# The last five MLP tiles and the entry of an S5 state space: an order written by hand, a separate residual buffer, a small position table, and a second period's positions issued ahead

## The chip, the cores and the metric

The kernel runs on one core of a Trainium2 chip. The metric is the device time of one execution in microseconds, median over runs. A core has a matrix engine (TensorE, PE in the profile), a vector engine (DVE), a scalar engine with function tables (ACT), GpSimd (POOL) and SyncE (SP), which in this kernel issues the transfers (DMA). Each engine runs its own instructions in the order in which the program lists them, and stands where one of them waits for another engine or a transfer. SBUF is the on-chip memory that the large buffers U, FD, H and W are cut from; PS is the matrix engine's accumulator memory, in banks of 512 fp32 columns.

## The reference

Two layers over 1024 latent tokens and 256 context tokens of width 1024, all in fp32. Layer 0 is a differential attention with a squared-ReLU MLP, layer 1 a bidirectional S5 state space with the same kind of MLP. The change lies at the border between them: the end of layer 0's MLP and the start of layer 1's mixer.

```
# end of layer 0                                   # start of layer 1
x = x + g2 * rmsnorm(mlp(h), norm_g[0, 3])         h_lat = rmsnorm(x, norm_g[1, 0]) * (1 + s1) + sh1
                                                   y = s5_mixer(h_lat, h_ctx, ...)
# s5: per group of 16 channels, a diagonal complex recurrence over time, forward and backward
lam_bar = exp(lam * dt);   h[t] = lam_bar * h[t-1] + b_bar @ u[t];   y[t] = real(c @ h[t])
```

## The kernel before

The 1280 tokens (8 latent tiles of 128, 0 to 7, and 2 context tiles, 8 and 9) go through MLP0's second product in `mlp0_down`: 53 blocks over 112 slices of the inner width, each product as three matrix instructions of 512 columns (`mm3`, L132 to L134). Partial sums are collected in FD (`yacc`, one 4 KB piece per tile), and half of the tiles is finished from the accumulators. Block 52 holds the last eight slices (q from 104 to 111) for five pairs of tiles, in which the tiles 9, 4, 5, 6, 7 come to their end.

A tile's end is the list of steps that `m0_tile` returns. `first` squares the half in the accumulator on ACT (L1712) and multiplies it by the gate row G on DVE (L1713). `root1` takes the reciprocal root on POOL. `residual` (L1726) adds the old residual x, loaded from xa, and stores the new one to xb in four transfers; it is written over the tile's sum y in FD. `second` squares that on ACT (L1731) and multiplies it by row A, on DVE or, for tiles 9 and 5, on POOL (L1732). `root` takes the second root. `modulate` (L1735) writes the result for layer 1 back into y. Then `transposed` (L1694, four quarters for a pair of tiles) turns it into U, from which the S5 reads.

In block 52 these steps are put in by `stages` and `advance`, which issue them in rounds, and the program's scheduler (`schedule_with_timeline_sim`) then reorders each engine's list by its own estimate of times.

The S5 (`s5`) runs 16 periods of 4 pairs of channel groups, for both directions d. A period n makes `phase(n, d)` (a sum of two integer tables, POOL, L1793), `trig(n, d)` (four steps on ACT, L1797 to L1800: the sine and cosine of the position), `inputs` (PE, L1813), `rotate` (two products on DVE, L1822, from the accumulators with the cosine and sine), a sum of both on POOL (L1903 forward, L1912 backward), `scan` (DVE, L1831), `back` (the rotation back, DVE or POOL, L1839) and `outputs` (PE). The scheduler is off here (`self.manual()`) for PE, ACT, DVE and POOL: they run in the written order. The positions of period 0 come from two small tables A0 and B0 (40 KB in all), those of later periods from a large one, ptd of 1664 KB, at FD 42.5. The `stages` calls of the tiles and the S5's opening are separate pieces of code, but run into one another on every engine. An offset such as FD 12 counts KB per partition.

Of the kernel before, what the change touches and what calls it, by code (L numbers as in the profile page):

```python
# [70 lines left out]
class Prog:  # L71
# [1525 lines left out]
    def mlp0_down(self):  # L1597
# [6 lines left out]
        self.bg = [self.s5_phases(40), self.s5_tables(0, self.bank(3), self.bank(2))]  # L1604

# [16 lines left out]
        for blk in range(53):  # L1622
            for q in range(112):
                d = q // 2 - blk
                if q > 3 and (d == 3 or blk == 0 and d < 3):
                    self.mlp0_load(q)
            for q in range(4 if blk == 0 else 2 * blk + 4, min(2 * blk + 6, 112) if blk < 52 else 112):
                self.mlp0_prep(q)
            steps = range(2 * blk, 2 * blk + 2) if blk < 52 else range(104, 112)
            n = steps[0] // 16  # L1630
            if blk == 40:
                self.drain()
                self.mlp0_rows(0)
                for i in range(4):
                    self.stages(self.m0_tile(i), 2)
                for pr in (0, 1):
                    self.stages([lambda pr=pr, c=c: self.transposed(pr, c) for c in range(3)])
            if blk == 48:
                self.advance()
                self.mlp0_rows(1)  # L1640
                self.stages(self.m0_tile(8), 2)
            if blk == 52:
                self.advance()
                for pr in (0, 1):
                    self.transposed(pr, 3)
                for t in range(5):
                    self.m0_early(T[t][1])
            for t in range(5):
                for q in steps:
                    products(q, t)  # L1650
                if steps[-1] % 16 == 15:
                    evac(n, t)
                if blk == 52:
                    i, b = T[t][1:]
                    fns = self.m0_tile(i, self.bank(b))
                    if i in (9, 5, 7):
                        pr = i // 2
                        fns += [lambda pr=pr, c=c: self.transposed(pr, c) for c in range(4)]
# [13 lines left out]
    def m0_buffers(self, i):  # L1672

        f, w = lambda x: self.fv(x, 1024), lambda: self.wv(12, 1024)
        h = lambda: self.hv(52, 1024).bitcast(F32)
# [20 lines left out]
    def m0_tile(self, i, b=None):  # L1696
# [9 lines left out]
        def first():  # L1706
            self.tile_dma(self.xa, i, x)
            if b is None:
                act.activation(junk, y, AF.Square, scale=1.0 / 32, accum_out=ms)
                pool.tensor_tensor(w, y, G, ALU.mult)  # L1710
                return
# [13 lines left out]
        def residual():  # L1725
            v.scalar_tensor_tensor(y, w, r, x, ALU.mult, ALU.add)  # L1726
            if i < 8:
                self.tile_dma(self.xb, i, y, store=True)

        def second():  # L1730
            act.activation(junk, y, AF.Square, scale=1.0 / 32, accum_out=ms)  # L1731
            (pool if i in (9, 5) else v).tensor_tensor(w, y, A, ALU.mult)  # L1732

        def modulate():
            v.scalar_tensor_tensor(y, w, r, B, ALU.mult, ALU.add)  # L1735

        return [first, root1, residual, second, root, modulate]
# [13 lines left out]
    def s5(self):  # L1751
# [14 lines left out]
        cs = [[(self.fv(x, 4, 128), self.fv(y, 4, 128)) for x, y in (((5, 32), (29.5, 34)), ((15, 22.5), (17.5, 22.5)))[d]]  # L1766
# [91 lines left out]

        for t, c0, w in ((A0, 0, 10), (B0, 5 * KB, 16)):
            self.dma(t, self.ptd[:, c0 : c0 + 128 * w].rearrange("p (d x w) -> p d x w", d=2, w=w)[:, :, 0:4])  # L1860

        load_x(0)
        self.dma(self.fv(42.5, 13 * KB).bitcast(I32), self.ptd)
        load_w(0)
        self.act_set("silu_and_others")
        with self.manual():
            act.activation(U[:, :, 160:192], U[:, :, 0:32], AF.Copy)
# [3 lines left out]
            phase(0, 0)  # L1871
            phase(0, 1)
            trig(0, 0)
            decay(0, 0)
            load_x(1)
            load_w(1)
            for n in range(19):
# [9 lines left out]
                if run:  # L1887
                    trig(n, 1)
                    decay(n, 1)
# [19 lines left out]
                if run:  # L1909
# [299 lines left out]
    def run(self):  # L2209
        tc = self.tc  # L2210
        pool = lambda name, **kw: tc.tile_pool(name=name, bufs=1, **kw)
        with pool("cst") as self.cst, pool("psp", space=bass.MemoryType.PSUM) as psp, \
# [53 lines left out]
            with pool("u") as up, pool("fd") as fp:  # L2266
                self.U, self.F = up.tile([128, 62 * KB], F32, name="U"), fp.tile([128, 56 * KB], F32, name="FD")
                self.mlp0_down()
                self.s5()
# [52 lines left out]
```

## Time and profile before

| what | number |
|---|---|
| time, median of 3 runs | 2897.81 us (2890.6 to 2905.84) |
| profiled execution, its own time | 2912.55 us |
| its span | 2910.8 us |
| granted TensorE clock, mean | 0.979 |
| busy: PE, DVE, ACT, POOL | 2747.0, 2024.0, 1366.7, 1070.7 us |
| last product of MLP0 starts | 1844.43 us |
| first product of the S5 starts | 1865.91 us |

The profile is of one execution. A timeline row gives the start, the duration, the engine, the line, the operation and its operands (out<-in), the count, and in brackets how long the engine stood idle before it and what ended that. The chain of waits follows back from the last instruction what each step waited for; its rows are start, length and the engine or transfer. A window's row gives the busy time of each engine in a stretch, the clock granted to TensorE, the share in which the DMA engines were busy, and GB/s.

### The profile page before, as it was taken

The numbers are of one execution on the slowest core, as the hardware profiler recorded it, in microseconds if no ns is written. First come the engines' busy times: TensorE is split into PE (matmuls) and PEld (weight loads), VectorE is DVE, ScalarE is ACT, GpSimd is POOL, SyncE is SP. The second block draws the span as 40 slices with busy tenths as digits, with TensorE's granted clock in tenths as the row PEclk, the third lists the DMA queues.
The fourth block names the chain that finished last, engine by engine and source line by source line (L and its number), as shares of the span: only waits on it lengthen the run. The fifth ranks groups of instructions, "written<-read, shape, count | busy, mean of one in ns | idle before, by whom it ended". The sixth has DMA issues, their size and how long they took to land.

```text
span 2910.8 us, 43626 instructions
## 1 busy us (share of the span) xinstructions
PE 2747.0 (94%) x15201; PEld 2296.5 (79%) x15201; DVE 2024.0 (70%) x2957; ACT 1366.7 (47%) x2556; POOL 1070.7 (37%) x923
## 2 busy tenths in 40 slices
PE   7999999999899999999999899689899899999999
PEld 4687888888777887878777788588788688888887
DVE  5456788777863667766787767699633687758566
ACT  3425555565554743333443435477443543345443
POOL 2314666666663600000100013699220543326324
PEclk9999999999999999999999999899999999999999
DMA  9855555555826468875899877578743254467544
GB/s 299 299 172 168 151 176 172 169 167 164 253 86 192 120 213 310 309 281 187 283 293 275 261 236 224 160 223 282 255 136 107 67 184 157 149 214 254 163 135 142
DMA packets 452010, 588.43 MB, mean 202 GB/s; under 512 B 60622, under 2 KB 297420, under 8 KB 448588
## 3 DMA queue, kind: packets, MB, share of 16 engines
q1 hardware_dynamic: 451788, 585.63, 63.4%
q8 instruction: 120, 1.97, 0.3%
q14 instruction: 102, 0.84, 0.1%
HBM read 398.47 MB, written 182.82 MB: 200 GB/s over the span
## 4 chain that ended last, share of the span: by engine, by line
PE 67%; DMA 12%; DVE 9%; issue 5%; POOL 3%; ACT 3%; SPq 2%; DVEq 0%; ACTq 0%; POOLq 0%
PE PS L132 19%; PE PS L134 19%; PE PS L133 18%; PE PS L523 3%; PE PS L569 2%; SPq L80 2%; PE PS L1813 2%; DMA FU<-in_mlp_w 2%; DMA Ta<-FU 1%; PE PS L1848 1%; DMA U<-Aa 1%; DVE H L138 1%; ACT F L546 1%; PE PS L202 1%; DVE F L557 1%
## 5 line engine op out<-in xcount | busy, mean ns | idle before, releaser
L132 PE MATMUL PS<-H 128*128 128x512 f32 x1048 | 413.8, 396 | 5.8 <-DVE FD L1620 4.0
L134 PE MATMUL PS<-H 128*128 128x512 f32 x1048 | 411.2, 393 | 1.3 <-DVE H L138 1.3
L133 PE MATMUL PS<-H 128*128 128x512 f32 x1048 | 412.0, 393 | 0.0
L132 PE MATMUL PS<-H,R 128*128 128x512 f32 (+1 forms) x836 | 309.6, 376 | 0.7 <-ACT H L137 0.7
L133 PE MATMUL PS<-H,R 128*128 128x512 f32 (+1 forms) x836 | 305.1, 365 | 4.2 <-POOL H L138 4.1
L134 PE MATMUL PS<-H,R 128*128 128x512 f32 (+1 forms) x836 | 303.8, 364 | 0.0
L132 PEld LDWEIGHTS PS<-H 128*128 128x128 f32 x1048 | 198.8, 190 | 51.1 <-DVE FD L1620 4.2
L134 PEld LDWEIGHTS PS<-H 128*128 128x128 f32 x1048 | 198.6, 190 | 44.4 <-DVE H L138 1.7
L133 PEld LDWEIGHTS PS<-H 128*128 128x128 f32 x1048 | 198.8, 190 | 41.5 <-issue 1.2
L137 ACT ACTIVATE R<-W 128x512 fp32r<-128x512 f32 (+1 forms) x199 | 139.0, 705 | 183.3 <-PE PS L133 119.1
L546 ACT ACTIVATE F<-F,stat 128x1280 f32<-128x1280 f32 x128 | 174.3, 1362 | 99.5 <-DVE F L536 99.3
L132 PE MATMUL PS<-R,H 128*128 128x512 f32 x532 | 213.0, 402 | 1.6 <-ACT R L137 1.6
L133 PE MATMUL PS<-R,H 128*128 128x512 f32 x532 | 210.5, 396 | 0.0
L134 PE MATMUL PS<-R,H 128*128 128x512 f32 x532 | 208.8, 396 | 0.0
L137 ACT ACTIVATE H<-U 128x640 fp32r<-128x640 f32 x216 | 133.0, 677 | 156.6 <-PE PS L133 123.6
L138 DVE TENSOR_TENSOR H<-W,H 128x512 fp32r<-128x512 f32 (+1 forms) x137 | 130.1, 960 | 90.6 <-ACT H L137 90.6
L138 DVE TENSOR_TENSOR H<-U,H 128x640 fp32r<-128x640 f32 x216 | 161.3, 783 | 43.1 <-ACT H L137 42.8
L536 DVE TENSOR_SCALAR_CACHE_REDUCE F<-PS 128x1280 f32<-128x1280 f32 x128 | 185.2, 1483 | 8.2 <-PE PS L523 7.9
L138 DVE TENSOR_TENSOR R<-W,R 128x512 fp32r<-128x512 f32 (+1 forms) x164 | 146.2, 899 | 62.9 <-ACT R L137 55.3
L583 POOL TENSOR_SCALAR R<-F 128x256 fp32r<-128x256 f32 (+1 forms) x128 | 128.0, 1000 | 148.7 <-ACT F L582 130.8
L133 PEld LDWEIGHTS PS<-H,R 128*128 128x128 f32 x836 | 161.3, 193 | 26.9 <-POOL H L138 5.9
L132 PEld LDWEIGHTS PS<-H,R 128*128 128x128 f32 x836 | 160.4, 192 | 26.5 <-issue 4.1
(491 smaller groups left out, 6850.5 us busy)
## 6 DMA issues: line engine op xcount, KB each, us to landing
W<-in_mlp_w SPq DMA_DIRECT2D x184, 256.0 KB, 3.0
U<-Aa SPq DMA_DIRECT2D x108, 320.0 KB, 4.5
Aa<-FU SPq DMA_DIRECT2D x91, 320.0 KB, 4.8
Ad<-F SPq DMA_DIRECT2D x112, 256.0 KB, 2.0
W<-Ad SPq DMA_DIRECT2D x112, 256.0 KB, 2.8
FU<-in_mlp_w SPq DMA_DIRECT2D x32, 512.0 KB, 5.5
Ta<-FU SPq DMA_DIRECT2D x16, 1024.0 KB, 4.4
recd<-U SPq DMA_DIRECT2D x64, 256.0 KB, 4.3
```

The costliest lines, as they stand in the source:

```text
L80: return self.nc.sync.dma_start(out=out, in_=in_)
L132: mm(out, ah, bh, start=first, stop=False, **kw)
L133: mm(out, ah, bl, start=False, stop=False, **kw)
L134: mm(out, al, bh, start=False, stop=last, **kw)
L137: self.nc.scalar.activation(hi, src, AF.Copy)
L138: (lo_eng or self.nc.vector).tensor_tensor(lo, src, hi.bitcast(F32), ALU.subtract)
L523: mm(self.PS[:, 1280 * c + k0 : 1280 * c + k1], Q[:, c, r, qs], K[c][:, k0:k1], start=r == 0, stop=r == 1)
L536: ts(p[c], self.PS[:, 1280 * c : 1280 * c + 1280], 1.0, None, ALU.mult, ALU.min, accum_out=sm[:, c : c + 1])
L546: nc.scalar.activation(p[c], p[c], AF.Exp, bias=sm[:, c : c + 1], scale=-1.0, accum_out=sn[:, 0:1] if c else s0[:, u + 1 : u + 2])
L569: self.nc.tensor.transpose(tb[:, 128 * (kt - k0) : 128 * (kt - k0) + 128], w[:, 128 * kt : 128 * kt + 128], self.ident)
L583: nc.gpsimd.tensor_scalar(hi, t, 1.0, 0.0, ALU.mult, ALU.add)
L1813: mm(b[:, o : o + 160], X[:, d, i, 64 * j : 64 * j + 128], U[:, 4 * n + i, cols], start=True, stop=True)
```

## The change

Block 52 no longer goes through `stages` and `advance`. `mlp0_end` makes a list `do` of pairs of a time and a function, for the five tiles in the order 9, 4, 5, 6, 7, at 5.4 apart, sorts it, and calls the functions inside `self.manual()`. So the order of PE, ACT, DVE and POOL is set by that list.

The residual stands apart: `residual` writes into w instead of y, the store reads w, `second` writes its product into y, and `modulate` works in y in place. Each of the last five tiles gets its own buffers (`m0_buffers`); the x of tiles 9, 4 and 5 are loaded ahead, those of 6 and 7 after the transposes of tile pair 4 (the context tiles). Tile 7's x is at FD 36 and its w, the source of its store, at FD 12 to 16. Its modulate is cut into four quarters, each followed by a transpose. `warm` puts 4, 5 and 3 products of the identity, into a part of bank 7, behind the last product.

`s5` becomes a generator. Its first part loads A0 and B0 (now at H 78 and 79) and hands four functions to `mlp0_end`: `positions(d)` = trig(0, d), `wrap` (a copy of U's first columns), `tables` (the load of the large table) and `places` = phase(0, 0) and phase(0, 1). The rest runs where `s5` was called. The load of ACT's function table moves from `s5` to the head of `mlp0_down`. In the S5's opening, decay(0, 1) (the decay rates, ACT) and phase(1, 0), trig(1, 0) and decay(1, 0) are issued ahead of period 0 instead of in it. The buffers of the phases and of the forward rotation (`ts`, `cs`) move: the second phase pair from 7.5 to 5, the forward rotation's first buffer from FD 5 to FD 10.

```diff
 in mlp0_down:
+        self.act_set("silu_and_others")
...
-                for t in range(5):
-                    self.m0_early(T[t][1])
+                self.mlp0_end(products)
+                continue
...
-                if blk == 52:
-                    i, b = T[t][1:]
-                    fns = self.m0_tile(i, self.bank(b))
...
-                    self.stages(fns, 2)
-                    self.advance(6)
 in m0_buffers:
-                8: lambda: (f(52), w()), 9: lambda: (h(), f(52)), 4: lambda: (w(), f(0)), 5: lambda: (h(), f(4)),
-                6: lambda: (w(), f(8)), 7: lambda: (h(), f(12))}[i]()
+                8: lambda: (f(52), w()), 9: lambda: (f(52), f(4)), 4: lambda: (h(), w()),
+                5: lambda: (u(52), u(48)), 6: lambda: (f(32), u(56)), 7: lambda: (f(36), f(12))}[i]()
 in m0_tile:
         def residual():
-            v.scalar_tensor_tensor(y, w, r, x, ALU.mult, ALU.add)
+            v.scalar_tensor_tensor(w, w, r, x, ALU.mult, ALU.add)
             if i < 8:
-                self.tile_dma(self.xb, i, y, store=True)
+                self.tile_dma(self.xb, i, w, store=True)
         def second():
-            act.activation(junk, y, AF.Square, scale=1.0 / 32, accum_out=ms)
-            (pool if i in (9, 5) else v).tensor_tensor(w, y, A, ALU.mult)
-
-        def modulate():
-            v.scalar_tensor_tensor(y, w, r, B, ALU.mult, ALU.add)
+            act.activation(junk, w, AF.Square, scale=1.0 / 32, accum_out=ms)
+            (pool if i in (9, 5) else v).tensor_tensor(y, w, A, ALU.mult)
+
+        def modulate(c=slice(0, 1024)):
+            v.scalar_tensor_tensor(y[:, c], y[:, c], r, B[:, c], ALU.mult, ALU.add)
+    def warm(self, n, after=None):
+        o = self.bank(7)[:, 384:512]
+        if after is not None:
+            self.nc.tensor.matmul(o[:, 0:1], self.ident, after, start=True, stop=True)
+        for _ in range(n):
+            self.nc.tensor.matmul(o, self.ident, self.ident, start=True, stop=True)
+    def mlp0_end(self, products):
+        T = ((8, 9, 0), (0, 4, 1), (1, 5, 4), (2, 6, 5), (3, 7, 6))
+        self.s5_run = self.s5()
+        positions, wrap, tables, places = next(self.s5_run)
+        for t in range(5):
+            self.m0_early(T[t][1])
+        load = lambda *i: [self.tile_dma(self.xa, j, self.m0_buffers(j)[0]) for j in i]
+        load(9, 4, 5)
...
+            at = 5.4 * t
+            do += [(at, lambda t=t: [products(q, t) for q in range(104, 112)]), (at + 5.45, first), (at + 6.7, root1),
...
+        with self.manual():
+            for _, f in sorted(do, key=lambda e: e[0]):
+                f()
 in s5:
-        A0, B0 = self.hv(46, 2, 4, 10).bitcast(I32), self.hv(47, 2, 4, 16).bitcast(I32)
-        phs = [(self.fv(x, 4, 160), self.fv(x + 2.5, 4, 160)) for x in (0, 7.5, 24.5)]
-        ts = [[(self.fv(x, 4, 160), self.fv((12.5, 20)[d], 4, 160)) for x in ((5, 29.5), (15, 17.5))[d]] for d in range(2)]
+        A0, B0 = self.hv(78, 2, 4, 10).bitcast(I32), self.hv(79, 2, 4, 16).bitcast(I32)
+        phs = [(self.fv(x, 4, 160), self.fv(x + 2.5, 4, 160)) for x in (0, 5, 24.5)]
+        ts = [[(self.fv(x, 4, 160), self.fv((12.5, 20)[d], 4, 160)) for x in ((10, 29.5), (15, 17.5))[d]] for d in range(2)]
...
+        yield positions, wrap, lambda: self.dma(self.fv(42.5, 13 * KB).bitcast(I32), self.ptd), places
         load_x(0)
-        self.dma(self.fv(42.5, 13 * KB).bitcast(I32), self.ptd)
         load_w(0)
-        self.act_set("silu_and_others")
         with self.manual():
-            act.activation(U[:, :, 160:192], U[:, :, 0:32], AF.Copy)
...
-            phase(0, 0)
-            phase(0, 1)
-            trig(0, 0)
             decay(0, 0)
+            decay(0, 1)
             load_x(1)
             load_w(1)
+            phase(1, 0)
+            trig(1, 0)
+            decay(1, 0)
             for n in range(19):
...
                 if run:
-                    trig(n, 1)
-                    decay(n, 1)
+                    if n:
+                        trig(n, 1)
+                        decay(n, 1)
...
-                    if n == 0:
-                        phase(1, 0)
-                        trig(1, 0)
-                        decay(1, 0)
```

Line numbers after the change: L1706 is the old L1713, L1719 the old L1726 (residual), L1725 the old L1732 (second's product), L1728 the old L1735 (modulate), L1687 the old L1694 (transposes), L1825 the old L1793 (phase), L1854 the old L1822 (rotate), L1863 the old L1831 (scan), L1871 the old L1839 (back), L1944 and L1953 the old L1903 and L1912 (the sums on POOL), L1845 the old L1813 (inputs), L1909 the old L1870 (zeroing a column of the decay rates).

Three places show how the order moves. The first is DVE, from tile 7's residual to the S5's first scan. Before:

```order
L1726 SCALAR_TENSOR_TENSOR FD<-FD,tl,H 128x1024 [waits DMAHW6_49,DMAHW5_49,DMAHW7_49,DMAHW4_49,Pool_49]
L1694 STREAM_TRANSPOSE U<-FD 128x16x32 [waits DVE_49]
L1694 STREAM_TRANSPOSE U<-FD 128x16x32 x3
L1732 TENSOR_TENSOR FD<-FD,W 128x1024 [waits DVE_49]
L1735 SCALAR_TENSOR_TENSOR FD<-FD,tl,W 128x1024 [waits DMAHW5_49,DMAHW6_49,DMAHW4_49,DMAHW7_49,Activation_49,Pool_49]
L1735 SCALAR_TENSOR_TENSOR FD<-FD,tl,W 128x1024 [waits DMAHW3_49,DMAHW2_49,DMAHW4_49,DVE_49,DMAHW5_49,Activation_49,Pool_49]
L1694 STREAM_TRANSPOSE U<-FD 128x16x32 [waits DVE_49]
L1694 STREAM_TRANSPOSE U<-FD 128x16x32 x3
L1822 TENSOR_TENSOR FD<-PS,FD 128x640 [waits PE_49] x2
```

And after, from tile 7's second product on:

```order
L1725 TENSOR_TENSOR FD<-FD,W 128x1024 [waits DVE_49]
L1687 STREAM_TRANSPOSE U<-FD 128x16x32 x2
L1728 SCALAR_TENSOR_TENSOR FD<-FD,tl,W 128x256 [waits DVE_49,Pool_49]
L1687 STREAM_TRANSPOSE U<-FD 128x16x32 [waits DVE_49]
L1728 SCALAR_TENSOR_TENSOR FD<-FD,tl,W 128x256
L1687 STREAM_TRANSPOSE U<-FD 128x16x32 [waits DVE_49]
L1728 SCALAR_TENSOR_TENSOR FD<-FD,tl,W 128x256
L1687 STREAM_TRANSPOSE U<-FD 128x16x32 [waits DVE_49]
L1728 SCALAR_TENSOR_TENSOR FD<-FD,tl,W 128x256
L1854 TENSOR_TENSOR FD<-PS,FD 128x640 [waits DMAHW3_49,DMAHW4_49,DMAHW2_49,DMAHW5_49,PE_49,Activation_49]
L1687 STREAM_TRANSPOSE U<-FD 128x16x32 [waits DVE_49]
L1687 STREAM_TRANSPOSE U<-FD 128x16x32 x2
```

The waits on transfers (DMAHW) leave the modulate; the first rotation, L1854, has four of them, which are the four parts of tile 7's store, and three transposes stand behind it.

The second is SyncE's list from the large table on. Before, up to the load behind it that belongs to tile 6:

```order
L80 DMA FD<-ptd 128x3328 [waits DMAHW4_49,DVE_49]
L80 DMA xb_77<-FD 32x1024 [waits DMAHW5_49,DVE_49]
L80 DMA xb_77<-FD 32x1024 [waits DMAHW6_49]
L80 DMA xb_77<-FD 32x1024 [waits DMAHW7_49]
L80 DMA xb_77<-FD 32x1024 [waits DMAHW0_49]
L80 DMA W<-xa_75 32x1024 [waits DMAHW1_49]
```

After, the rows around tile 7's store, which stands behind the S5's first matrices, at the end of the list's part for the tiles:

```order
L80 DMA xb_77<-U 32x1024 [waits DMAHW4_49,DVE_49]
L80 DMA xb_77<-U 32x1024 [waits DMAHW5_49]
L80 DMA xb_77<-U 32x1024 [waits DMAHW6_49]
L80 DMA xb_77<-U 32x1024 [waits DMAHW7_49]
L80 DMA W<-recd 64x1024 [waits DMAHW0_49]
L80 DMA H<-recd 128x1536 [waits DMAHW1_49]
L80 DMA xb_77<-FD 32x1024 [waits DMAHW2_49,DVE_49]
L80 DMA xb_77<-FD 32x1024 [waits DMAHW3_49]
L80 DMA xb_77<-FD 32x1024 [waits DMAHW4_49]
L80 DMA xb_77<-FD 32x1024 [waits DMAHW5_49]
L80 DMA W<-recd 128x1536 [waits DMAHW6_49,DVE_49,Pool_49]
```

The table's load heads the stretch in both, and the store of tile 7 (from FD) ends it; tile 6's store now reads U, and the matrices stand between them in another order.

The third is POOL around period 0 of the S5. Before:

```order
L1793 TENSOR_TENSOR FD<-H 128x640 [waits DVE_49]
L1903 TENSOR_TENSOR FD<-FD 128x640 [waits DVE_49]
L1912 TENSOR_TENSOR FD<-FD 128x640 [waits DMAHW6_49,DMAHW7_49,DMAHW0_49,DVE_49]
L1793 TENSOR_TENSOR FD<-FD 128x640 [waits DMAHW6_49,DMAHW7_49,DMAHW5_49,DMAHW4_49]
L1839 TENSOR_TENSOR FD<-FD 128x512 [waits DVE_49]
L1793 TENSOR_TENSOR FD<-FD 128x640 [waits Pool_49]
```

After:

```order
L1909 MEMSET U 128x4 [waits DMAHW6_49,DMAHW7_49,DMAHW5_49,DMAHW4_49]
L1909 MEMSET U 128x4 x2
L1825 TENSOR_TENSOR FD<-FD 128x640 [waits DVE_49]
L1944 TENSOR_TENSOR FD<-FD 128x640 [waits DMAHW4_49,DMAHW3_49,DMAHW5_49,DMAHW2_49,DVE_49]
L1953 TENSOR_TENSOR FD<-FD 128x640 [waits DVE_49]
L1871 TENSOR_TENSOR FD<-FD 128x512 [waits DVE_49]
L1825 TENSOR_TENSOR FD<-FD 128x640 [waits Pool_49]
```

The phase of period 1 (the L1793 that read FD, behind L1912) now stands ahead of the first sum, behind the zeroing instructions, of which the first waits for tile 6's store.

More of the change, by code (lines that the diff above doesn't have):

```diff
@@ L1737, in m0_tile @@
-        return [first, root1, residual, second, root, modulate]
+            act.activation(junk, w, AF.Square, scale=1.0 / 32, accum_out=ms)
+            (pool if i in (9, 5) else v).tensor_tensor(y, w, A, ALU.mult)
+        def modulate(c=slice(0, 1024)):
+            v.scalar_tensor_tensor(y[:, c], y[:, c], r, B[:, c], ALU.mult, ALU.add)
+        fns = [first, root1, residual, second, root, modulate]
+        return fns if b is None else (fns, r)
+    def warm(self, n, after=None):
[4 more added lines that the diff above has]
+            self.nc.tensor.matmul(o, self.ident, self.ident, start=True, stop=True)
@@ new lines, in mlp0_end @@
+    def mlp0_end(self, products):
[6 more added lines that the diff above has]
+        load(9, 4, 5)
+        do = []
+        for t in range(5):
+            i, b = T[t][1:]
+            (first, root1, residual, second, root, modulate), r = self.m0_tile(i, self.bank(b))
+            at = 5.4 * t
+            do += [(at, lambda t=t: [products(q, t) for q in range(104, 112)]), (at + 5.45, first), (at + 6.7, root1),
+                   (at + 7.8, residual), (at + 9.1, second), (at + 10.4, root)]
+            if i == 7:
+                do += [(at + 11.4 + 0.1 * c, lambda c=c: (modulate(slice(256 * c, 256 * c + 256)), self.transposed(3, c)))
+                       for c in range(4)]
+                do += [(at + 5.41, lambda: self.warm(4)), (at + 6.8, lambda: self.warm(4, r)), (at + 10.5, lambda: self.warm(2, r))]
+            else:
+                do.append((at + 11.5, modulate))
+        do += [(13.3, lambda: [self.transposed(4, c) for c in (0, 1)]), (13.4, tables),
+               (14.6, lambda: ([self.transposed(4, c) for c in (2, 3)], load(6, 7))),
+               (17.6, places), (22.5, lambda: positions(0)), (27.9, lambda: positions(1)),
+               (30.8, lambda: [self.transposed(2, c) for c in (0, 1)]), (31.8, wrap),
+               (34.0, lambda: [self.transposed(2, c) for c in (2, 3)])]
+        with self.manual():
+            for _, f in sorted(do, key=lambda e: e[0]):
+                f()
@@ L1762, in s5 @@
         At, Bt = self.fv(42.5, 128, 10).bitcast(I32), self.fv(47.5, 128, 16).bitcast(I32)
[L1763 to L1766 removed]
+        A0, B0 = self.hv(78, 2, 4, 10).bitcast(I32), self.hv(79, 2, 4, 16).bitcast(I32)
+        phs = [(self.fv(x, 4, 160), self.fv(x + 2.5, 4, 160)) for x in (0, 5, 24.5)]
+        ts = [[(self.fv(x, 4, 160), self.fv((12.5, 20)[d], 4, 160)) for x in ((10, 29.5), (15, 17.5))[d]] for d in range(2)]
+        cs = [[(self.fv(x, 4, 128), self.fv(y, 4, 128)) for x, y in (((10, 32), (29.5, 34)), ((15, 22.5), (17.5, 22.5)))[d]]
               for d in range(2)]
@@ L2268, in run @@
                 self.mlp0_down()
-                self.s5()
+                for _ in self.s5_run:
+                    pass
                 for g in range(2):
```

14 lines of the change are left out of this document (9 added, 5 removed).

## The prediction, made before the result was known

> **What bounds the kernel now.** I read the chain of waits first, around the end of the last MLP0 block, then the timelines of PE, DVE, SyncE and POOL over the same 60 us, then the transfers and the windows. The chain through the change's place, start and length in us:
>
> ```profile
> core 0 of [0], span 2910.8 us
> 1852.75 8.47 DMA xb<-FD
> 1861.34 1.30 DVE FD L1735
> 1862.70 1.27 POOL FD L1793
> ...
> 1876.34 1.72 POOL FD L1793
> 1880.55 1.61 POOL FD L1793
> 1882.18 0.74 ACT FD L1797
> ```
>
> So between the MLP and the state space (S5) the path is: a store of a residual tile to xb (tile 6), a modulate that waits for it, positions (L1793) on POOL, and then POOL's work of period 0, with the positions of period 1 (1876.34, 1880.55) in it, on which ACT's sines (L1797) wait. What that costs TensorE is in its timeline:
>
> ```profile
> 1844.20 0.39 PE L133 MATMUL PS<-H 128*128 128x512 f32 x1
> 1844.43 0.39 PE L134 MATMUL PS<-H 128*128 128x512 f32 x1
> 1865.91 6.80 PE L1813 MATMUL PS<-U,H 128*128 128x160 f32 x32 [21.09 <-DVE U L1694]
> ```
>
> PE stands for 21.09 us from the last product (ends at 1844.82) to the first S5 product. DVE's rows show why, and when the S5 gets going:
>
> ```profile
> 1827.13 1.28 DVE L1726 SCALAR_TENSOR_TENSOR FD<-FD,tl,H 128x1024 f32<-128x1024 f32 x1 [0.36 <-POOL tl L144]
> ...
> 1832.24 1.28 DVE L1735 SCALAR_TENSOR_TENSOR FD<-FD,tl 128x1024 f32<-128x1024 f32 x1 [1.14 <-POOL tl L144]
> ...
> 1845.63 0.69 DVE L1713 TENSOR_TENSOR FD<-PS,W 128x512 f32<-128x512 f32 x1 [1.10 <-ACT PS L1712]
> ...
> 1850.30 1.22 DVE L1732 TENSOR_TENSOR FD<-FD,W 128x1024 f32<-128x1024 f32 x1
> ...
> 1863.82 1.28 DVE L1735 SCALAR_TENSOR_TENSOR FD<-FD,tl,W 128x1024 f32<-128x1024 f32 x1 [1.20 <-DMA xb<-FD]
> 1865.14 2.49 DVE L1694 STREAM_TRANSPOSE U<-FD 128x512 f32<-128x512 f32 x4
> 1868.44 0.82 DVE L1822 TENSOR_TENSOR FD<-PS,FD 128x640 f32<-128x640 f32 x1 [0.81 <-PE PS L1813]
> ...
> 1873.56 1.48 DVE L1831 TENSOR_TENSOR_SCAN FD<-U,FD 128x640 f32<-128x640 f32 x1
> ...
> 1885.11 1.56 DVE L1822 TENSOR_TENSOR FD<-PS,FD 128x640 f32<-128x640 f32 x2 [2.54 <-ACT FD L1800]
> ```
>
> Two dates carry the argument: tile 7's store has landed at 1863.8, when its modulate is let go, and the first rotation of the S5 (L1822; L1854 in the new code), call it R, starts at 1868.44. From R on, the S5 runs at the pace of DVE and POOL (last row below: 19.51 and 19.64 busy of 20), so what R gains stays gained to the end. The stores are late since a full queue stands ahead of them:
>
> ```profile
> 1833.56 0.34 SPq L80 DMA_DIRECT2D FD<-ptd  x1
> ...
> 1857.69 3.96 SPq L80 DMA_DIRECT2D xb<-FD  x4
> FD<-ptd SPq DMA_DIRECT2D x1, 1664.0 KB
> xb<-FD SPq DMA_DIRECT2D x16, 128.0 KB, 7.4
> H<-recd SPq DMA_DIRECT2D x2, 768.0 KB
> 1834.00:1868.00 34.00, 12.91 (x56) 10.73 (x55) 22.50 (x26) 17.25 (x26) 15.47 (x17) 0.73 0.92 282
> 1835.00:1840.00 5.00, 5.00 (x24) 4.14 (x23) 4.76 (x7) 3.77 (x5) 2.44 (x4) 1.00 0.91 318
> 1900.00:1920.00 20.00, 15.53 (x115) 15.05 (x115) 19.51 (x19) 14.38 (x23) 19.64 (x12) 0.95 0.72 222
> ```
>
> (The windows' columns are length, busy us of PE, PE loads, DVE, ACT, POOL, then granted clock, DMA share, GB/s.) From the issue of the large table ptd at 1833.56 to the landing of tile 7's store, SyncE puts in 1664 (ptd) + 4 x 512 (stores of tiles 4 to 7) + 1024 (tiles 6 and 7 in) + 40 + 3328 (S5 matrices, by their shapes) = 8104 KB; they take 1863.8 - 1833.56 = 30.2 us, 274 GB/s, at a share of 0.92.
>
> **The change, part by part.**
>
> *Order by hand.* Tile 9's eight products, 24 instructions 0.227 us apart (the two PE rows), now come in a row at the head of the block; counted back from 1844.43 by four tiles (96 instructions), tile 9's last starts at 1822.65 and ends at 1823.0. Before, its square started later:
>
> ```profile
> 1825.36 0.58 ACT L1712 ACTIVATE PS<-PS 128x512 f32<-128x512 f32 x1 [6.20 <-PE PS L134]
> ```
>
> So tile 9 runs 2.3 us earlier, if nothing else holds it, and its modulate ends at 1831.2 in place of 1833.5. PE's sum of work is the same: its last product still ends at 1844.8.
>
> *The end of the tile chain.* For tile 7: tile 6's residual ends between 1842.5 (its products end at 1839.4, and tile 9 took 3.05 from its square to its residual's end) and 1845.1 (with tile 5's multiply and modulate ahead on DVE); I take the later. Then ACT's two squares, 1.2 and 0.8, to 1847.1; on DVE 0.69 + 1.28 (modulate of 6) + 1.28 + 1.22 + two transposes at 0.62 end at 1852.8, four quarters of the last modulate (between 0.32, a quarter of 1.28, and 0.69, the 512-wide row; I take 0.4, nearer to the quarter) and three transposes end at 1856.3. The first quarter's transpose lets PE start at about 1853.9: 12.0 us earlier than 1865.91. All of it is shorter since *the residual stands apart*: modulate now writes another buffer than the one which the store reads, so the waits of L1735 on xb (the 8.47 in the chain, and 1.20) are gone.
>
> *What is late next.* The residual's buffer of tile 7 is FD 12 to 16, and R now writes FD 10 to 12.5 (the rotation's buffers moved from 5 to 10). So R, which had no such wait, takes the wait for tile 7's store (in the order its row has the four DMA semaphores). Behind R on DVE stand three transposes of tiles 5 and 7, POOL's sum L1944 and everything after. What stands ahead of the store is almost what stood there: 1664 + 4 x 512 + 1024 + 3328 = 8064 KB against 8104, by the same queue. At the same rate it takes 30.1 us from the table's issue, which follows tile 9's modulate: 1831.2 + 30.1 = 1861.3. R then starts at 1861.4, not at 1856.4 where DVE would be ready. Gain at R: 1868.44 - 1861.4 = **7.0 us**: 2.3 from the earlier table load, and 4.7 since before the modulate, four transposes and a product came between the landing and R. Bounds: at 318 GB/s, the best 5 us of the stretch (row of 1835), 8064 KB take 26.0 us, R 1857.3, gain 11.1; from the landing of tile 6's store (7080 KB in the 27.8 us from 1833.56 to 1861.34) the rate is 261 GB/s, R 1862.9, gain 5.5. I take 274, since it is for the same store.
>
> The Trainium skill (DMA: Bandwidth & Descriptors, Queues, rings and completion order) says that each DMA engine takes descriptors in ring order; by it the store can't pass the loads that stand ahead, as the 8.47 in the chain bears out.
>
> From R to the scan the length stays: before 1873.56 - 1868.44 = 5.1; after, four rotations at 0.82 and three transposes at 0.62, 5.1.
>
> *Second period's positions ahead.* phase(1,0) leaves POOL's place between L1912 and L1839 in period 0 (1.72 on the chain at 1876.34) for the time in which POOL waits for R. The second pair of rotations of period 1 (1885.11, after 2.54 of waiting for a sine that hangs on POOL) comes by that much sooner. Bounds: 1.7, the row, and 2.5, the wait; I take **2.1**, the middle, as no row tells which of DVE and ACT ends first. On POOL the positions stand behind zeroing instructions (L1909) that now wait for tile 6's store; 6528 KB are queued up to its end, 24.4 us, so it lands at 1855.6, before R: nothing. DVE and POOL both keep the lead, as what follows is their own work.
>
> *First positions from a small table, table of ACT's functions at the head.* The 40 KB are loaded long before, the trigonometry of period 0 runs in ACT's gaps, and one load of functions in place of two goes where ACT waits for PE anyway:
>
> ```profile
> 1850.35 1.28 ACT L1797 ACT_TABLE_LOAD   x1
> 1856.22 1.28 ACT L141 ACT_TABLE_LOAD   x1
> ```
>
> Both stood beside the wait for xb; cover: without it they would be worth at most 2.6. Nothing. The 12 small products that keep PE busy (bank 7) come after the last MLP0 product, while PE would stand; nothing, and up to 0.4 (one product's row) if the last of them held the first S5 product.
>
> *Sum.* 7.0 + 2.1 = 9.1 us. The profiled execution took 2912.55 for its span of 2910.8; it becomes 2903.4. It lies 14.7 above the median shown, 2897.81, which becomes **2889**. The three runs span 2890.6 to 2905.84, so about 0.5% (14.5 us) is what can be told from no change.
>
> **Rivals.**
>
> A. The store isn't what holds R: it lands before DVE is ready at 1856.3. R is then 1856.4, gain 12.0 + 2.1 = 14.1, time 2883.7. For it: 318 GB/s over 5 us is near. Against it: the queue would have to move 8064 KB in 25.1 us, 329 GB/s, for the whole stretch, where the mean was 282. The Trainium skill (the same page, Where 436 GB/s comes from) gives about 358 GB/s as what HBM allows one core: by that, an estimate, the store lands at 1854.3 and rival A holds. The trace's best row of 318 stays 11% under that.
>
> B. Slower: the same queue drains worse, and R, which now waits for the store, comes later than before. The page's mean over the whole span:
>
> ```profile
> DMA packets 452010, 588.43 MB, mean 202 GB/s; under 512 B 60622, under 2 KB 297420, under 8 KB 448588
> ```
>
> At 202 GB/s 8064 KB take 40.9 us, R at 1872.2, 3.8 later than before, less 2.1: 1.7 slower, 2899.5. It decides when the store lands over 39.3 us after the table's issue (R past 1870.5). For it: tiles 6 and 7 are now loaded through the same queue, and a store that SyncE issues in order may be late. Against: the share stood at 0.92 over the 34 us from 1834, with much the same transfers.
>
> C. The positions ahead are worth nothing: rotation (1,0) on DVE or x of period 1, which lands about 2.9 us after the store, sets period 1. Gain 7.0, time 2890.8; or the gain at R runs into a slack later in the S5, gain 3 to 5, 2893 to 2895. The DVE row of 1900 to 1920 speaks against slack.
>
> **How the numbers follow.** Forecast (gain 7.5 to 12, store sets R) 0.50; rival A 0.20; C, with its gains from 3 to 7, 0.19; B and small losses 0.11. The forecast and A reach from 2884 to 2890; C to 2895; B 2899.5. A median of three moves by some 5 us more, so 2879 to 2899 holds 8 in 10. Faster by over 0.5% wants 14.5 us: most of half of A, and the upper scatter of the forecast: 0.17. Slower by over 0.5% is further than B's price and wants B with a slow draw of runs: 0.07. The rest, 0.76, is within 0.5%.
>
> **What would show it.** The first S5 product near 1854 and no wait of L1728 on xb: the residual apart. A wait of DVE L1854 on a DMA to xb of about 5 us, ending near 1861: the store holds R; no such wait, A; ended past 1870, B. No L1825 between L1953 and L1871 in period 0, and the second pair of rotations of period 1 some 14.6 us behind R, where it was 16.7 before: positions ahead. One load of functions. The prediction is wrong if the time up to 1844 moves, if PE's last MLP0 product ends elsewhere, or if the S5's later periods change their length.

## The result, and the profile after

The changed kernel takes 2894.99 us (median of 20 runs, 2877.45 to 2900.76), the kernel before, run beside it 20 times, 2904.18 us. The ratio between the runs is 0.9971, with a 95% interval of 0.9959 to 0.9983: 8.4 us shorter, by the interval 4.9 to 11.9 (the two medians alone differ by 9.2). Forecast were 9.1 us, a ratio of 0.9969, and a time within 0.5% of the one before; all three hold. The forecast of 2889 was counted from a median of 2897.81 over three runs, which over 20 is 6.4 higher.

The profiled execution took 2899.15 us, its span 2897.4. Of the 13.4 us by which that span is shorter than the one before, only a part belongs to the change: the last MLP0 product already stands 7 us earlier. The prediction had named that product's moving as a sign that it is wrong. But the profiles of the runs below end it anywhere from 1830.8 to 1843.5, and two of them whose code up to there is the changed kernel's own at 1837.0 (e10 in the table below) and 1843.5 (e1), so a single profile's 7 us says nothing about the change. All dates below are therefore counted from the end of the last MLP0 product, which is 1844.82 in the profile before and 1837.85 in this one. TensorE's timeline:

```profile
1837.45 0.40 PE L134 MATMUL PS<-H 128*128 128x512 f32 x1
1837.68 1.06 PE L1738 MATMUL PS<-ident 128*128 128x128 f32 x8
1845.52 0.59 PE L1736 MATMUL PS<-tl,ident 128*128 128x1 f32 x2 [6.78 <-POOL tl L144]
1845.97 2.06 PE L1738 MATMUL PS<-ident 128*128 128x128 f32 x8
...
1851.01 6.55 PE L1845 MATMUL PS<-U,H 128*128 128x160 f32 x32
```

The first S5 product comes 13.2 us behind the last MLP0 product, in place of 21.1 (each dummy product stands as two in the rows, so eight stand for four). DVE's timeline, from tile 4's modulate on:

```profile
1830.88 2.34 DVE L1728 SCALAR_TENSOR_TENSOR FD<-FD,tl,W 128x1024 f32<-128x1024 f32 x1
1833.15 2.30 DVE L1719 SCALAR_TENSOR_TENSOR U<-U,tl 128x1024 f32<-128x1024 f32 x1
...
1841.05 1.28 DVE L1719 SCALAR_TENSOR_TENSOR U<-U,tl,FD 128x1024 f32<-128x1024 f32 x1 [0.84 <-POOL tl L144]
...
1853.10 0.44 DVE L1728 SCALAR_TENSOR_TENSOR FD<-FD,tl,W 128x256 f32<-128x256 f32 x1
1854.67 0.82 DVE L1854 TENSOR_TENSOR FD<-PS,FD 128x640 f32<-128x640 f32 x1 [1.12 <-DMA xb<-FD]
...
1859.67 2.82 DVE L1863 TENSOR_TENSOR_SCAN FD<-U,FD 128x640 f32<-128x640 f32 x1 [0.20 <-POOL FD L1944]
...
1869.73 1.79 DVE L1854 TENSOR_TENSOR FD<-PS,FD 128x640 f32<-128x640 f32 x2 [0.95 <-ACT FD L1832]
...
1948.03 1.54 DVE L1854 TENSOR_TENSOR FD<-PS,FD 128x640 f32<-128x640 f32 x2
```

The first rotation R (1854.67) waits for tile 7's store, as forecast, but for 1.12 us and not for 5: DVE itself is ready at 1853.54. The same place in the chain of waits, and SyncE's issues:

```profile
1848.95 5.59 DMA xb<-FD
1854.58 0.05 DVEq L1854
1854.67 0.82 DVE FD L1854
```

```profile
1824.75 0.34 SPq L80 DMA_DIRECT2D FD<-ptd  x1
...
1847.39 1.99 SPq L80 DMA_DIRECT2D xb<-FD  x4
```

From the table's issue to the landing of tile 7's store at 1854.54 pass 29.8 us (forecast 30.1). The row to set beside 1948.03, the rotations of period 8, is in the timeline before:

```profile
1963.22 1.54 DVE L1822 TENSOR_TENSOR FD<-PS,FD 128x640 f32<-128x640 f32 x2
```

So the S5 is 118.4 - 110.2 = 8.2 us ahead at period 8, and 8.3 at the end of the last product of its last period (225.3 and 217.0). From period 2 to period 8 pass 69.2 us in both kernels, so the later periods have kept their length. The end of the S5 is the coarser date: from period 8 to there the runs below take anything from 103.8 to 107.5 us.

### The profile page after: what moved, and what is told of

Read it like the earlier page. It is cut to its first block, busy times and chain, and to the rows that moved or that the text cites. A ratio compares the mean times of both kernels' runs of the same rounds, so it can differ in the third digit from the quotient of the medians.

```text
span 2897.4 us, 43677 instructions
## 1 busy us (share of the span) xinstructions
PE 2747.0 (95%) x15225; PEld 2296.1 (79%) x15225; DVE 2026.9 (70%) x2960; ACT 1362.4 (47%) x2555; POOL 1063.2 (37%) x923
```

## The experiments

All runs are read by the same dates, in us from the end of the last MLP0 product; the time of a single execution scatters by more than what is asked, so it isn't used. "DVE ready" is the end of the instruction ahead of R.

| run | DVE ready | R | first scan | period 8 |
|---|---|---|---|---|
| before | 22.8 | 23.6 | 28.8 | 118.4 |
| changed | 15.7 | 16.8 | 21.8 | 110.2 |
| changed again (e10) | 15.7 | 17.2 | 22.2 | 110.6 |
| rotations off the store (e1) | 15.7 | 15.7 | 20.7 | 109.1 |
| table loaded twice (e2) | 19.3 | 22.0 | 26.0 | 114.3 |
| positions of period 1 back (e3) | 15.7 | 16.2 | 21.2 | 110.5 |
| residual joined (e4) | 25.1 | 25.1 | 30.1 | 118.3 |
| kernel before, residual apart (e5) | 17.9 | 18.8 | 24.0 | 113.7 |
| no dummies (e6) | 15.7 | 18.0 | 23.0 | 111.4 |
| tile 7 earlier (e7) | 15.4 | 17.2 | 22.2 | 110.5 |
| and position sums earlier (e8) | 14.3 | 16.1 | 21.1 | 109.4 |
| and no dummies (e12) | 14.3 | 14.3 | 19.5 | 107.8 |
| and SyncE in written order (e9) | 14.3 | 14.3 | 20.1 | 108.4 |
| positions of period 0 late (e11) | 16.7 | 16.8 | 21.6 | 109.8 |

In e2 and e11 three transposes stand ahead of R that stand behind it elsewhere, so those two are read at the scan. The expectations of the first four runs counted from the end of the first dummy products, 1838.74; 0.9 is to be added to their dates.

**Rotations off the store.** Edit: the first two rotations of period 0 write elsewhere.

```
+        t_first = (self.fv(36, 4, 160), self.fv(38.5, 4, 160))
+        pair = lambda n, d: t_first if (n, d) == (0, 0) else ts[d][n % 2]
-            (Ps, Pc), (t1, t2) = phs[(2 * n + d) % 3], ts[d][n % 2]
+            (Ps, Pc), (t1, t2) = phs[(2 * n + d) % 3], pair(n, d)
...
```

> All dates are counted from the end of the last MLP0 product. In the changed kernel the first rotation R starts at 15.9, after 1.1 us of waiting for tile 7's store, with DVE ready at 14.8. Here the first two rotations of period 0 write FD 36 to 41, which tile 7's store doesn't read; all else stays. Theory (the store is what holds R last, by 1.1 us): no wait of DVE on xb, R at 14.8, and the S5 1 us earlier. Rival (the store's wait only covers another one, of PE or ACT): R stays at 15.9 with another name in the row.

The wait is gone and R follows DVE's list at once, 1.1 us earlier, and so does period 8. The theory holds: the store held R, by 1.1 us.

**Table loaded twice.**

```
+               (13.5, tables), (17.6, places),
```

> The large table is loaded twice, one right behind the other, so 1664 KB more stand ahead of tile 7's store; nothing else changes. Theory (R follows the store, and the store follows the bytes ahead of it at the 277 GB/s of the changed kernel's stretch): landing 6.2 us later, at 22.0, R at 22.1, DVE's wait on xb 7.3 us, the time 6 us longer. Rival 1 (the queue goes at the 401 GB/s of its last 5 us once it is full): 4.2 later, R at 20.1. Rival 2 (the queue isn't what dates the store): R stays within 1 us of 15.9.

The scan comes 4.2 us later and period 8 4.1. DVE waits twice:

```profile
DVE FD L1854 <- DMA xb<-FD: 2.6, 1, 2.6
DVE U L1719 <- DMA xb<-U: 2.5, 1, 2.5
```

R follows the queue, so rival 2 falls. The store landed some 35.0 us after the first table load, 5.2 more than in the changed kernel for 1664 KB more; that lies between the theory's 6.2 and rival 1's 4.2, and settles no rate. The second load didn't follow at once, either: SyncE issued it 7.3 us behind the first (1832.14 and 1824.85), with four stores and three of the eight loads of x between them. Part of the delay shows as another wait, of tile 6's residual (L1719) for a DMA. The row names a store, but that tile's x stands behind the second load too; which of them it was isn't shown.

**Positions of period 1 back in period 0.**

```
-            phase(1, 0)
-            trig(1, 0)
-            decay(1, 0)
             for n in range(19):
...
+                    if n == 0:
+                        phase(1, 0)
+                        trig(1, 0)
+                        decay(1, 0)
```

> The positions of period 1 go back to their place inside period 0, behind the second sum on POOL. Theory (they stood on POOL's path): R stays at 15.9, the second pair of rotations of period 1 starts 16.7 behind R, where it is 15.1 in the changed kernel, and the S5 ends 1.6 to 2.1 later. Rival (they lay in a gap of POOL): the second pair stays 15.1 behind R, and nothing changes.

The second pair of rotations of period 1 starts 15.9 behind R, where it is 15.1 in the changed kernel and 16.7 before. From the first scan to period 8 pass 89.3 us with the positions back, 88.4 in the changed kernel (88.35 and 88.39 in its two profiles), 89.7 before. All eleven profiles with the move lie between 88.2 and 88.4, so 0.9 is far outside their scatter. The move is worth 0.9, neither the theory's 1.6 nor nothing.

**Residual joined.**

```
-            v.scalar_tensor_tensor(w, w, r, x, ALU.mult, ALU.add)
+            v.scalar_tensor_tensor(y, w, r, x, ALU.mult, ALU.add)
-                self.tile_dma(self.xb, i, w, store=True)
+                self.tile_dma(self.xb, i, y, store=True)
...
```

> The residual is written over y again, and stored from y, and modulate writes y: only this part of the change is undone, the order by hand and the rest stay. Theory (modulate waited for the store of its own tile): waits of L1728 on xb come back, for tile 6 some 4 us and for tile 7 as well, R at 20 to 21 in place of 15.9, the time 4 to 5 longer. Rival (in the order by hand the stores land early enough): R within 1 us of 15.9.

R is at 25.1, 8.3 later than in the changed kernel and later than before; the theory had 21 to 22 in these dates. The waits of this run on DVE:

```profile
DVE FD L1728 <- DMA xb<-FD: 12.4, 4, 4.3
```

Four modulates wait for their store, for 3.1, 3.7, 4.3 and 1.2 us: each holds up the residual behind it, whose store then starts later. The expectation counted 4 to 5 us in all; the waits add up to 12.4, and R comes 8.3 later. The rival falls.

**The kernel before with the residual apart**: the same two functions and buffers of `m0_tile` as in the change, in the old code.

```
-            v.scalar_tensor_tensor(y, w, r, x, ALU.mult, ALU.add)
+            v.scalar_tensor_tensor(w, w, r, x, ALU.mult, ALU.add)
...
-            v.scalar_tensor_tensor(y, w, r, B, ALU.mult, ALU.add)
+            v.scalar_tensor_tensor(y, y, r, B, ALU.mult, ALU.add)
```

> The kernel before with one part of the change: the residual written to its own buffer and stored from there, modulate in place; order by scheduler, buffers, tables and S5 as before. Dates from the end of the last MLP0 product, where the kernel before has R at 23.6 and the changed kernel at 16.8 (the expectations of the four runs ahead counted from the end of the first dummy products, 0.9 later). Theory (undoing this part in the changed kernel cost 8.3 us at R, so it carries the gain): the waits of L1735 on xb go, 5 to 6 us of R's 23.6 with them, R at 17.5 to 19. Rival (a wait takes their place: the pairs of tiles that share a work buffer, W 12 for tiles 4 and 6 and H 52 for 5 and 7, now wait for the store that reads it): R at 23 or later.

R is at 18.8, 4.8 us earlier than before, and period 8 as well; the theory holds, the rival falls. None of the groups of waits on DVE in this stretch is a wait for xb any more; the largest that remain are:

```profile
DVE FD L1713 <- ACT PS L1712: 10.3, 4, 4.6
DVE FD L1735 <- POOL tl L144: 3.2, 4, 1.1
```

This part alone carries 4.8 of the 8.2 us. The order by hand and the rest bring 2.0 at R and 3.5 at period 8 on top, and without this part (e4) 1.5 less than nothing at R.

**No dummies.**

```
-                do += [(at + 5.41, lambda: self.warm(4)), (at + 6.8, lambda: self.warm(4, r)), (at + 10.5, lambda: self.warm(2, r))]
```

> The changed kernel without the 12 dummy products. In its profile the granted clock fell to 0.50 in spite of them, and the first 32 S5 products took 6.55 us against 6.80 before. Theory (they neither hold the clock nor stand on the path): R stays at 16.8 within 0.6, the scan at 21.8 within 0.6. Rival (they hold a part of the clock that R's products need): R 0.5 to 2 us later.

DVE is ready at 15.7 as before the edit. R is at 18.0 and the scan at 23.0, both 1.2 later than the theory allowed for its 0.6, since the store landed later in this profile:

```profile
DVE FD L1853 <- DMA xb<-FD: 2.3, 1, 2.3
```

The rival's 0.5 to 2 us of loss is there by the number, but not by its cause: what R waits for is the store, not PE, although the first 32 S5 products take 7.24 us here and 6.55 with the dummies. Why the store landed later isn't known; in four profiles with the same list on DVE up to R (changed, e10, e3, e6) R is at 16.8, 17.2, 16.2 and 18.0. The clock rows of the changed kernel (below) are 0.63, 0.50 and 0.50 with the dummies there; over the same three windows this run has 0.71, 0.50 and 0.50 without them.

**Tile 7 earlier.** Beside the first run's edit:

```
+            if i == 7:
+                do += [(22.2, first), (22.95, root1), (25.35, residual), (26.0, second), (27.8, root)]
```

> The changed kernel with the first two rotations of period 0 off tile 7's store (as in the first run), and tile 7's square, first product and residual moved ahead of tile 6's modulate in the list. Theory (R is then set by the order on DVE and ACT): DVE is ready 1.2 us earlier than 15.7, R at 14.3 to 14.9, the S5 2 us earlier than in the changed kernel. Rival (tile 6's root on POOL sets it): R stays at 15.7.

DVE is ready 0.35 earlier and not 1.2, and R is later, at 17.2: DVE waits 1.8 us for PE, where the dummy products now stand ahead of the first S5 product (14.7 in place of 13.2). Neither theory nor rival.

**And the position sums earlier.**

```
-               (17.6, places)
+               (12.2, places)
```

> The run before it, with the two position sums of period 0 (POOL) moved ahead of tile 5's second product to where POOL stood idle for 2.65 us. In the changed kernel tile 4's modulate and tile 5's residual took 2.34 and 2.30 us on DVE, beside these sums (3.49 for two where 2.54 is their time), in place of 1.28 each. Theory (the two engines hold each other up over shared reads): both come back to 1.28, one other DVE instruction grows, R 1 us earlier than in the run before. Rival (the 2.3 is the instruction's own, from its operands in U): they stay at 2.3, R stays.

The theory holds in its durations. DVE's rows of this run, with tile 4's residual, then tile 4's modulate and tile 5's residual:

```profile
1824.28 2.29 DVE L1719 SCALAR_TENSOR_TENSOR W<-W,tl,H 128x1024 f32<-128x1024 f32 x1 [0.85 <-POOL tl L144]
...
1830.61 1.26 DVE L1728 SCALAR_TENSOR_TENSOR FD<-FD,tl,W 128x1024 f32<-128x1024 f32 x1
1831.80 1.27 DVE L1719 SCALAR_TENSOR_TENSOR U<-U,tl 128x1024 f32<-128x1024 f32 x1
```

The long one is whichever stands beside POOL's sums. DVE is ready 1.1 earlier than in e7. R still waits 1.84 for PE behind the dummies.

This run also bears on what dates tile 7's store. In the changed kernel its issue (1847.39) follows the end of tile 7's residual (1847.36) at once, so either the residual or the queue could hold it. Here the residual ends 3.2 us earlier, 6.4 behind the last product, and the store is issued later, at 11.1 where it was 9.5:

```profile
1841.63 1.28 DVE L1719 SCALAR_TENSOR_TENSOR FD<-FD,tl 128x1024 f32<-128x1024 f32 x1
...
1847.65 4.44 SPq L80 DMA_DIRECT2D xb<-FD  x4
```

So an earlier residual doesn't bring the store forward: SyncE's transfers in front of it hold it. The run with SyncE in written order (below) shows the same from the other side.

**And no dummies** (the edits of e8 and e6 together):

> The first run of this call without the change of SyncE's order: tile 7 and the position sums earlier, rotations off the store, no dummies. Theory: DVE ready at 14.3 and R there; the scan at 19.3, and the second pair of rotations of period 1 held by POOL's zeroing instruction, which waits for tile 6's store, so some 0.5 to 1 us of it is lost again by period 1. Rival (PE's wait for x sets R): R at 15.5 or later.

R is at 14.3 and the scan at 19.5, as said; period 8 at 107.8 is the earliest of all, 10.6 us ahead of the kernel before. The loss that was expected from the zeroing instructions isn't there: the second pair of period 1 comes 9.9 behind the scan, against 10.1 in the changed kernel.

**And SyncE in written order**:

```
-        load_w(0)
+        with self.tc.manual_schedule(engines={..., nc.sync.engine}):
...
             load_x(1)
+            load_w(0)
             load_w(1)
```

> The run with tile 7 and the position sums earlier, now also without the dummy products (in it they stood in front of the first S5 product) and with SyncE's list in the S5 in written order, so that the matrices of period 0's outputs (1280 KB) and period 2's x (768 KB) go behind tile 7's store. Dates from the end of the last MLP0 product. Theory (with store, position sums and dummies out of the way DVE's own list sets R): R at 14.3 against 16.8, the scan at 19.3 against 21.8, the S5 2.5 us shorter to its end; against the kernel before 10 to 11 us, a ratio of 0.996 to 0.9965. Rival (SyncE's fixed order makes later periods wait for loads): the scan as said, but the S5's end no earlier than 216.

Only 768 KB of the S5's matrices now stand in front of tile 7's store, where 3328 did (2560 less; the expectation had counted 2048), and SyncE issues it at 6.4, as soon as its residual has ended, where it was 11.1 in e8. R is at 14.3, but the scan at 20.1: two rotations wait 0.70 and 0.20 us, by the trace for ACT and PE; the cause was not followed. Period 8 is at 108.4, the S5's end at 212.1 against 217.0 and 216.0 in the changed kernel's two profiles; the rival falls. The time is 2890.81 us (12 runs, 2880.47 to 2895.71), 0.9959 of the kernel before's (0.9943 to 0.9975).

**The changed kernel again**, unedited:

> The changed kernel once more, beside the run before it on the same chip, for a direct comparison. Theory: a ratio near 0.997 to the kernel before, R at 16.8 within 1 (it was 16.2 to 18.0 in runs that left the store and the list on DVE alone).

Beside e9 on the same chip it is at 2893.71 us (11 runs), 0.9979 (0.9963 to 0.9996) of the same 23 runs of the kernel before, whose median is 2900.34. The two intervals overlap, so that e9 beats the changed kernel is shown by the dates (2 us at period 8) and not by the times; that it beats the kernel before is shown by both.

**Positions of period 0 late.**

```
-               (17.6, places), (22.5, lambda: positions(0)), (27.9, lambda: positions(1)),
+               (40.0, places), (40.1, lambda: positions(0)), (40.2, lambda: positions(1)),
```

> The changed kernel with the position sums and the sines of period 0 moved back behind the last transposes, into the S5's opening; the small table still comes early. Theory (they had room there: POOL is free from 11.7, and 1.3 and 2.9 us of sum and sines end at 15.8, where DVE is ready at 15.7; tile 4's modulate and tile 5's residual lose their neighbour, so DVE is ready earlier): R within 0.6 of 16.8. Rival (the early positions carry some of the gain): R or the scan 2 us or more later.

The scan is at 21.6 and period 8 at 109.8, both within 0.4 of the changed kernel's: in this profile, taking the first positions ahead gained nothing. Tile 4's modulate and tile 5's residual, with POOL's sums gone from beside them, are back at 1.27 and 1.28, as expected, and tile 6's residual behind them ends earlier:

```profile
1827.95 1.27 DVE L1728 SCALAR_TENSOR_TENSOR FD<-FD,tl,W 128x1024 f32<-128x1024 f32 x1
1829.13 1.28 DVE L1719 SCALAR_TENSOR_TENSOR U<-U,tl 128x1024 f32<-128x1024 f32 x1
...
1836.01 1.28 DVE L1719 SCALAR_TENSOR_TENSOR U<-U,tl,FD 128x1024 f32<-128x1024 f32 x1 [0.84 <-POOL tl L144]
```

It ends 2.4 behind the last product (1834.92) where it was 4.5. Part of that is lost again at tile 7's first two quarters of modulate, which now stand beside the sums and take 1.27 and 0.74 in place of 0.44. The small table itself was early in this run too, so its own part was not tried apart.

## Why the prediction was right, and where not

- **Table load earlier by 2.3.** The table is issued 13.1 us ahead of the end of the last product, where it was 11.3: 1.8 us. It follows the end of tile 9's modulate, as worked out, which lies 13.1 and not 13.6 ahead.
- **The store behind the same bytes.** 29.8 us for 8064 KB, where 30.1 were worked out. R at 16.8, where 1861.4 - 1844.8 = 16.6 stood. The gain at R is 6.8, where 7.0 stood. e1 shows that it is the store which holds R, e2 that R goes with the queue, and e8 and e9 that what is queued ahead holds the store, and not its residual alone. The prediction had the last point from the order in which a queue takes its work; the 8.47 that it named fits, but only these runs show it. That 29.8 and 30.1 lie so near is in part luck: from the table's issue to R, four profiles with the same transfers ahead have 29.3 (e3), 29.9 (changed), 30.3 (e10) and 31.1 (e6). The two small tables A0 and B0 are 40 and 64 KB, 104 in all and not 40; only the 40 KB stood behind the large table, so the sum of 8104 KB stands.
- **DVE ready at 1856.3 (11.5 in these dates): wrong.** It is 15.7, so the new wait costs 1.1 and not 5, and rival A's gain of 14 at most wasn't there to be had: with the wait gone (e1) R is at 15.7 and not at 11.5. The step that failed is tile 6's residual, which was to end between 1842.5 and 1845.1, at most 0.3 behind the last product. Its row (1841.05, 1.28) ends 4.5 behind it, 4.2 late; from there to DVE's readiness 11.2 us pass, as worked out. Ahead of it, tile 4's modulate and tile 5's residual took 2.34 and 2.30 in place of 1.28 each, beside POOL's sums, which the change puts there. With the sums moved away (e11) tile 6's residual ends 2.4 behind the last product, so these neighbours are 2.1 of the 4.2. The other 2.1 was not taken apart; what the rows show is that on ACT tile 6's square stands behind tile 5's second one, which waits for tile 5's residual. The first S5 product is late by nearly the same sum, 13.2 where 9.1 stood.
- **Residual apart.** As forecast the waits of modulate on xb are gone. Alone it is worth 4.8 (e5); undone in the new order it costs 8.3. That the sum had 4.7 for what stood between landing and R is a coincidence and no check of it, since R in e5 doesn't wait for the store.
- **Second period's positions, 2.1.** Mis-sized. From the scan to period 8 the changed kernel is 1.3 shorter; undoing this part alone gives back 0.9. The 0.4 left were not traced. The bounds, 1.7 and 2.5, took POOL's row for the path in full; 0.9 lies about midway between the lower bound and rival C, by which these positions are worth nothing.
- **First positions, function table, dummies, at nothing.** e11 and e6 bear out the first and the last as far as single profiles can: nothing is lost with the positions late, and DVE's date doesn't move without the dummies. The early position sums are not free, though: they are the neighbours that cost DVE the 2.1 us above, which the wait for the store hid. No load of the function table stands in ACT's rows of this stretch any more; that part was not tried alone.
- **The sum.** 9.1 were 7.0 and 2.1; measured are 6.8 to R, 6.9 to the scan and 8.2 by period 8, and 8.4 in the times. It came out close in part by luck: R was set by the store, whose date came from one row, so that the 4 us by which the date for DVE was missed stayed hidden behind it (with the store gone, as in e1, they show); and 1.3 us came between scan and period 8 in place of 2.1.
- **Rivals.** B would have needed the store past 25.7; it landed at 16.7. Rival A wanted 329 GB/s over the whole stretch; that rate was there at times, as the windows of the changed kernel show, but not throughout:

```profile
1840.00:1845.00 5.00, 0.00 (x0) 0.00 (x0) 3.44 (x5) 3.28 (x7) 2.06 (x6) 0.63 1.03 349
1845.00:1850.00 5.00, 2.99 (x13) 2.70 (x13) 4.97 (x6) 4.59 (x6) 1.33 (x6) 0.50 0.90 247
1850.00:1855.00 5.00, 5.00 (x20) 4.86 (x21) 3.77 (x8) 0.97 (x2) 1.41 (x1) 0.50 1.01 401
```

## What to carry to other kernels

Where a result is stored and then worked on in place, the next step waits for the store's landing, and here that came behind what was queued ahead. A second buffer took 4.8 us off an entry of 24 us, and it pays to ask at once which later step reuses that second buffer. A date that hangs on a queue came out within 1 us in four profiles, from the bytes ahead and the rate of the same stretch. A date from a hand-made list on several engines missed by 4 us, half of it because steps' durations were taken from places where the neighbour engine stood still. Fillers for an engine need a look too: dummies that waited for a late value stood, two experiments later, in front of the work that they were to help.

## What was not expected of the hardware

DVE and POOL hold each other up, by about a whole instruction at a time. In the changed kernel POOL's two sums, 1.27 each alone, took 3.49 while DVE's two instructions took 2.34 and 2.30 in place of 1.28; and a POOL instruction of 0.30 took 1.39 from the start of DVE's modulate of 1.29 on:

```profile
1817.74 0.30 POOL L1715 TENSOR_SCALAR tl<-tl 128x1 f32<-128x1 f32 x1
...
1823.43 1.29 DVE L1728 SCALAR_TENSOR_TENSOR FD<-FD,tl 128x1024 f32<-128x1024 f32 x1 [0.41 <-POOL tl L144]
1823.50 1.39 POOL L1715 TENSOR_SCALAR tl<-tl 128x1 f32<-128x1 f32 x1
...
1830.87 3.49 POOL L1825 TENSOR_TENSOR FD<-H 128x640 int32<-128x640 int32 x2
```

The Trainium skill (GPSIMD Engine Reference, Specifications) names the SBUF interfaces of GpSimd as shared with VectorE, with contention from VectorE instructions of two SBUF inputs. The rows agree in kind, since a modulate and a residual each read two buffers in SBUF, and e8 and e11 moved the delay with the neighbour.

The granted clock fell to 0.63 and 0.50 (windows above) although four dummy products followed the last one, and more came 6.8 us later; without any dummies (e6) it was 0.71 and 0.50.

The DMA engines moved 401 GB/s over the 5 us from 1850. The Trainium skill (DMA: Bandwidth & Descriptors, Where 436 GB/s comes from) has about 358 as the limit of HBM for one core, half of a stack's 716. The measurement decides: with one core running, as here, that figure is no ceiling for 5 us of loads and stores. Over the whole 29.8 us the mean was 277.
